# A two-block transformer kernel: the keys of differential attention projected 512 features at a time, and three smaller edits of pools and order

## The chip, the core and the metric

The kernel runs on one core of one Trainium2 chip. The metric is the device time of one execution in microseconds, as the median of several runs. TensorE (PE) multiplies, VectorE (DVE), ScalarE (ACT) and GpSimd (POOL) work element by element, and SyncE (SP) issues most of the transfers. Each engine runs its own list of instructions in order, and semaphores make one wait for another.

## The reference, cut to what matters

Two blocks follow each other on 512 tokens of 1024 features, all in fp32. The first is a DiT block: an RMS norm modulated by a condition, one input projection, a gated linear attention (GLA) and a differential attention side by side, an output projection, a second norm and a SwiGLU FFN. The second is a mixer block with a pooling and a "fox" attention branch, a cross attention to 256 memory tokens, and a FFN with a short convolution. The part that is projected differently here is `dk`, the keys of differential attention, for 256 context tokens and 512 tokens of x; the others keep their arithmetic.

```
def diff_qkv(parts, q_norm_g, k_norm_g):
    dq, dk, dv = parts[5:]
    ...
    k = rmsnorm(dk.reshape(b, n, DIFF_HEADS, 2, DIFF_DH).transpose(0, 2, 1, 3, 4), k_norm_g)
...
        x = x + gt1 * mix
        x = x + gt2 * swiglu(modulate(x, norm2_g[l], sh2, sc2), w_ffn_in[l], w_ffn_out[l])
```

## The kernel before, in words

Every large product is done as three matmuls on split operands (high by high, high by low, low by high). `wsplit` (L173) loads a chunk of 128x1024 weights into one of two `wf` buffers of a ring, casts its high part on ACT (L187) and subtracts the low part on DVE (L188); `whi` and `wlo` come from a small ring as well. A scheduler writes the order of each engine's list: by priorities, in the order in which the code issues work, with `tc.cur_priority` and `tc.issue_after` as corrections. Pools give memory, and a tile that takes the place of an older one waits for the older one's last reader.

The start is `normed_x` (L427): for four pairs of rows of x, ACT squares one into `t`, DVE squares the other into `u` and adds them (L433, L434), and PE sums over partitions (L313), with a few warming matmuls between. `t` has two buffers, `u` has one. Then come the modulation (L353), the spread of the norm factor (L332) and the first projections (L196 to L198).

The projections that have tokens as output rows are cut into tiles of 128 tokens by 256 features: `tm_job` (L674) loads the weights of half the features (two chunks) and runs 24 matmuls of 256 columns for each of six token tiles. For `dk` that is twelve tiles; after each, `qk_piece` (L648) squares and sums the heads and applies gains and rotation, and after the sixth tile of a half a factor `r_qk` is worked out and multiplied in (L692). All these tiles are entries of the list `fillers`. `mem_sq` (L725) lies between them: it loads a piece of the memory tokens into a buffer with the tag "t2", and squares into one with the tag "t1", which `qk_piece` uses too. The first entries are run ahead of the GLA stage, the last `PJ` = 20 between its steps. Where the stage opens, its constants `LT` and `Lr` are loaded through the two `wf` buffers and cast on DVE (L828, L831).

Norm 2 (L1323) runs behind the output projection for two halves of the tokens: it sums squares on PE, works out the factor and spreads it, in steps that lie between pieces of projection (`yield`). Behind the mixer's cross attention, `post` (L1434) adds its normed result, held in `KV` for the second half of the tokens, to `X` (L1453). The second FFN's pool `fp2` then takes the place of the pools `xp` and `xt`, of which `KV` is a tile. `Fhi` and `Flo` in `fp2` take split weights first (L187, L188), later split results.

Of the kernel before, what the change touches and what calls it, by code (L numbers as in the profile page):

```python
# [20 lines left out]
S = 512  # L21
# [7 lines left out]
RW = 1088  # L29
GH = 0  # L30
FA, FG, FC, A0, GR, MU = 3.4, 2.5, 5.6, 2, 2, 12
PJ, FP = 20, 8
NF = 2
NWF = 2
T0 = 1
# [11 lines left out]
QP = (0,)  # L47
Q3 = 0
MG = 1
WU, WX, WW = 15, 1, 5  # L50
MV, W0 = (0, 1), 1
XG = 9
ML = 0
W4, W5 = 1, 1
W1, W2 = 2, 2
X2 = (0, 2, 4)
XR, DR = (1, 3, 5, 7), (1, 3, 5, 7)
# [23 lines left out]
def kernel(ctx: ExitStack, tc: tile.TileContext, a: dict, out: bass.AP, stop=None):  # L81
# [307 lines left out]
    with tc.tile_pool(name="st", bufs=1) as st, tc.tile_pool(name="st2", bufs=2) as st2:  # L389
# [37 lines left out]
        def normed_x(x):  # L427

            pt = mis()
            for k in range(0, KT, 2):  # L430
                t, u = (st2.tile([128, S], F32, tag=f"sqt{j}", name="sqt", bufs=2 - j) for j in range(2))
                A.activation(t, x[:, k], AF.Square)
                V.tensor_tensor(u, x[:, k + 1], x[:, k + 1], ALU.mult)  # L433
                V.tensor_tensor(u, u, t, ALU.add)  # L434
                with tc.issue_after(warm(WU if k == 0 else WX)):
                    last_warm[0] = sum_sq(pt, u, k == 0, k == KT - 2)
            yield
            rb = st.tile([128, S], F32, tag="rbx", name="rbx")
# [206 lines left out]

    sums_of = {}

    def qk_piece(p, dst, gname, rope_t, key, i, n):  # L648


        if i == 0:
            sums_of[key] = mid2.tile([128, n, 4], F32, tag="qss", name="qss")
        sq = mid2.tile([128, 256], F32, tag="t1", name="qsq")
        A.activation(sq, p, AF.Square)  # L654
        V.tensor_reduce(sums_of[key][:, i], sq.rearrange("p (h e) -> p h e", h=4), AX, ALU.add)
        d4, p4 = dst.rearrange("p (h e) -> p h e", h=4), p.rearrange("p (h e) -> p h e", h=4)
        if rope_t is None:
            V.tensor_tensor(d4, p4, r_(gname).rearrange("p (o d) -> p o d", o=1).to_broadcast([128, 4, 64]), ALU.mult)
            return
        t2 = mid2.tile([128, 4, 2, 32], F32, tag="t2", name="t2")  # L660
        cs = cs64
        V.tensor_tensor(d4, p4, cs[:, 0, rope_t].rearrange("p (o d) -> p o d", o=1).to_broadcast([128, 4, 64]), ALU.mult)
        V.tensor_tensor(t2, p.rearrange("p (h y f) -> p h y f", h=4, y=2)[:, :, ::-1],
                        cs[:, 1, rope_t].rearrange("p (o y f) -> p o y f", o=1, y=2).to_broadcast([128, 4, 2, 32]), ALU.mult)
        V.tensor_tensor(d4, d4, t2.rearrange("p h y f -> p h (y f)"), ALU.add)

    def qk_rms(key, n):

        return rsqrt(mid2, sums_of[key].rearrange("p t h -> p (t h)"), 4 * n, 1.0 / 64, "qk")

    fillers = []
    got = {}
# [11 lines left out]
            take(hf, t, p[:, :256], slice(hf * 256, (hf + 1) * 256))  # L684
        return run

    def take_k(hf, t, p, cs):
        qk_piece(p, kn[:, t, cs], "k_g", None if t < 2 else t - 2, "k", t, 6)
        if t == 5:
            r = qk_rms("k", 6)  # L690
            k4 = kn[:, :, cs].rearrange("p t (h e) -> p t h e", h=4)
            V.tensor_tensor(k4, k4, r.rearrange("p (t h o) -> p t h o", t=6, o=1).to_broadcast([128, 6, 4, 64]), ALU.mult)  # L692

    late = {}

# [13 lines left out]
        if t == 5:  # L709
            V.tensor_scalar(rq[:, :, 4 * hf:4 * hf + 4], qk_rms("q", 4).rearrange("p (t h) -> p t h", t=4), 0.125, None, ALU.mult)  # L710

    jobs = [("w_dk", hf, range(6), take_k) for hf in range(2)]
    jobs += [("w_dv", hf, range(2), take_v) for hf in range(2)]
    jobs += [("w_dq", hf, range(2, 6), take_q) for hf in range(2)]
    jobs += [("w_dv", hf, range(2, 6), take_v) for hf in range(2)]
    for w, hf, ts_, take in jobs:
        if (w, hf) == ("w_dv", 0) and len(fillers) == 12:
            fillers.append((0.0, turn_q))
        for t in ts_:
            fillers.append((1.45, tm_job(w, hf, t, take, t == ts_[0])))  # L720
# [16 lines left out]
        V.tensor_copy(rm, r)  # L737
        bcast(rbm, r)
    for k in range(KT):
        fillers.insert(2 * k + 1, (0.0, lambda k=k: mem_sq(k)))  # L740
    fillers.insert(2 * KT + 2, (0.5, mem_stats))
    got_rs = []

    def silu_r(m, x, y, p):
# [71 lines left out]

    fill_to(len(fillers) - PJ)
    late_by[0] = HO
    gla_scope = ExitStack()
    gp = gla_scope.enter_context(tc.tile_pool(name="gp", bufs=1))  # L820
    gt = gla_scope.enter_context(tc.tile_pool(name="gt", bufs=2))
# [346 lines left out]
        mnl = mlo[:, 4:8].rearrange("p k (u t) -> p (k u) t", u=2)  # L1168

    gd = midp.tile([128, 1], F32, name="gd")  # L1170
    V.tensor_scalar(gd, col("diff_norm_g", 0), 0.8, None, ALU.mult)

    def mem_in(k):
        m = ap2.tile([128, MEM], F32, tag="mk", name="mk")
# [148 lines left out]
    def norm2(x, y):  # L1323
        for _ in range(W4 if x else W5):
            yield
        r = fm_stats(sp, sqs[:, x:y], "n2")
        for _ in range(3 if x else 1):
            yield
        bcast(rb[:, x:y], r)
        for k in range(KT):  # L1330
            if k % 2:
                yield
            t = sp.tile([128, S // 2], F32, tag="n2t", name="n2t")
            V.tensor_tensor(t, X[k][:, x:y], rb[:, x:y], ALU.mult)
# [99 lines left out]
    def post(Y, gname, nextg, g2, tails, spread):  # L1434


        def ev(m, x, y, p):
            V.tensor_scalar(Y(m // 2 * 2, x, y)[:, m % 2], p, col(gname, m), None, ALU.mult)
            add_sq(p, m, x, y)

        def after(x, y):
            rbp = sp.tile([128, S // 2], F32, tag="rbp", name="rbp")
            r = fm_stats(sp, sqs[:, x:y], "post")
            yield
            bcast(rbp, r)
            yield
            rb2 = rbp.rearrange("p (o t) -> p o t", o=1).to_broadcast([128, 2, S // 2])
            held = hq.tile([128, 2, S // 2], F32, tag="hld", name="hld")
            for k in range(0, KT + 2, 2):
                if k < KT:  # L1450
                    y2, x2 = Y(k, x, y), XT[k // 4][:, k % 4:k % 4 + 2, x:y]
                    V.tensor_tensor(y2, y2, rb2, ALU.mult)
                    V.tensor_tensor(x2, x2, y2, ALU.add)  # L1453
                    for j in (k, k + 1):
                        A.activation(g2[0][:, j, x:y], X[j][:, x:y], AF.Copy, scale=col(nextg, j))
                    t = held if k == 0 else sp.tile([128, 2, S // 2], F32, tag="sqx", name="sqx", bufs=1)
                    A.activation(t, x2, AF.Square)
                    yield
                if k > 0:
                    for j in (k - 2, k - 1):  # L1460
                        V.scalar_tensor_tensor(g2[1][:, j, x:y], X[j][:, x:y], col(nextg, j), f32(g2[0][:, j, x:y]),
                                               ALU.mult, ALU.subtract)
                    if k > 2:
                        V.tensor_tensor(held, held, last, ALU.add)
                    yield
                if k < KT:
                    last = t

            def tail():
# [213 lines left out]
    xa = ExitStack()  # L1683
    xp = xa.enter_context(tc.tile_pool(name="xp", bufs=1))
    xt = xa.enter_context(tc.tile_pool(name="xt", bufs=2))
    KV = xp.tile([128, 8, MEM], F32, name="KV")
    KVM, VM = KV[:, 0:4], KV[:, 4:8].rearrange("p (t u) n -> p t (u n)", t=2)
    g4 = new_q()
    Ym = xp.tile([128, KT, S], F32, name="Ym")
# [213 lines left out]
def _layout(i):  # L1903
# [68 lines left out]
```

## Time and profile before

| what | value |
|---|---|
| median of 3 runs | 1642.4 us (1641.32 to 1644.54) |
| the profiled execution: its time, its span | 1641.52 us, 1639.1 us |
| mean granted clock of PE over the span | 0.989 |
| DVE busy, ACT busy | 948.0 us (58%), 718.7 us (44%) |
| SP's queue of transfers | 158.15 MB |

The span is from the first to the last instruction; 2.4 us of the execution's time lie around it. Shares are of the span.

### The profile page before, as it was taken

How to read it: one execution, taken by the hardware profiler on the slowest of the kernel's cores; microseconds unless marked ns; L12 is line 12 of the kernel's file. 1: busy time of each engine (PE TensorE's matmuls, PEld its weight loads, DVE VectorE, ACT ScalarE, POOL GpSimd, SP SyncE). 2: the span in 40 equal slices, each digit the busy share in tenths (PEclk: the TensorE clock that was granted, in tenths of full speed). 3: DMA queues.
4: the chain of work that ended last, by engine and by line, in shares of the span. 5: the costliest groups of instructions: out<-in, count | busy, mean ns of one | idle time of the engine just before them, and what ended most of it. 6: DMA issues, size and time to landing. Idle time of an engine off the chain costs nothing.

```text
span 1639.1 us, 25459 instructions
## 1 busy us (share of the span) xinstructions
PE 1590.6 (97%) x10098; PEld 1355.6 (83%) x10098; DVE 948.0 (58%) x1791; ACT 718.7 (44%) x1353; POOL 214.1 (13%) x237
## 2 busy tenths in 40 slices
PE   7999999999999999999999999999998999999997
PEld 5798977778889888888889777888988988888887
DVE  5626898788765222223335676445788777776333
ACT  3424555677645323232223565224466544444221
POOL 0300000111022122210004000122000222221001
PEclk8999999999999999999999999999999999999999
DMA  8232245332322333333332212234211233323332
GB/s 350 82 89 78 66 158 180 124 100 78 128 88 78 103 94 99 91 99 94 93 114 72 77 39 65 91 103 148 84 52 34 83 93 100 103 90 97 97 93 74
DMA packets 49046, 163.23 MB, mean 100 GB/s; under 512 B 5664, under 2 KB 11296, under 8 KB 47392
## 3 DMA queue, kind: packets, MB, share of 16 engines
q1 hardware_dynamic: 45328, 158.15, 30.4%
q10 hardware_dynamic: 3312, 3.18, 0.6%
q8 instruction: 79, 1.29, 0.3%
q0 software_dynamic: 288, 0.28, 0.1%
q14 instruction: 39, 0.32, 0.1%
HBM read 158.72 MB, written 3.15 MB: 99 GB/s over the span
## 4 chain that ended last, share of the span: by engine, by line
PE 85%; DVE 5%; ACT 3%; DMA 1%; issue 1%; POOL 0%; ACTq 0%; DVEq 0%; POOLq 0%
PE acc L197 16%; PE acc L198 16%; PE acc L196 16%; PE s L198 5%; PE s L196 5%; PE s L197 5%; PE acc L286 3%; PE acc L285 3%; PE acc L287 3%; PE mis L1147 1%; PE mis L1632 1%; DVE wlo L188 1%; PE acc L775 1%; PE s L1118 1%; DMA mk<-in_memT 1%
## 5 line engine op out<-in xcount | busy, mean ns | idle before, releaser
L187 ACT CAST whi<-wf 128x1024 fp32r<-128x1024 f32 (+4 forms) x221 | 228.6, 1034 | 422.6 <-PE acc L197 277.7
L188 DVE TENSOR_TENSOR wlo<-wf,whi 128x1024 fp32r<-128x1024 f32 (+2 forms) x183 | 222.0, 1213 | 176.2 <-ACT whi L187 172.3
L196 PE MATMUL acc<-qhi,whi 128*128 128x512 f32 (+1 forms) x640 | 239.4, 374 | 0.0
L197 PE MATMUL acc<-qlo,whi 128*128 128x512 f32 (+1 forms) x640 | 239.3, 374 | 0.0
L198 PE MATMUL acc<-qhi,wlo 128*128 128x512 f32 (+1 forms) x640 | 239.3, 374 | 0.0
L196 PEld LDWEIGHTS acc<-qhi,whi 128*128 128x128 f32 x640 | 120.8, 189 | 19.6
L197 PEld LDWEIGHTS acc<-qlo,whi 128*128 128x128 f32 x640 | 120.7, 189 | 19.7 <-issue 0.2
L198 PEld LDWEIGHTS acc<-qhi,wlo 128*128 128x128 f32 x640 | 120.7, 189 | 19.3
L196 PE MATMUL s<-qhi,whi 128*128 128x512 f32 (+1 forms) x336 | 128.3, 382 | 0.0
L198 PE MATMUL s<-qhi,wlo 128*128 128x512 f32 (+1 forms) x336 | 128.3, 382 | 0.0
L197 PE MATMUL s<-qlo,whi 128*128 128x512 f32 (+1 forms) x336 | 128.2, 382 | 0.0
L188 POOL TENSOR_TENSOR wlo<-wf,whi 128x1024 fp32r<-128x1024 f32 x38 | 91.0, 2396 | 214.3 <-ACT whi L187 214.3
L1417 DVE TENSOR_TENSOR e<-e,s 128x512 f32<-128x512 f32 (+1 forms) x22 | 14.3, 651 | 154.2 <-PE s L198 154.1
L197 PE MATMUL acc<-glo,whi 128*128 128x512 f32 (+1 forms) x208 | 74.4, 358 | 0.1
L196 PE MATMUL acc<-ghi,whi 128*128 128x512 f32 (+1 forms) x208 | 74.4, 358 | 0.0
L198 PE MATMUL acc<-ghi,wlo 128*128 128x512 f32 (+1 forms) x208 | 74.2, 357 | 0.0
L196 PEld LDWEIGHTS s<-qhi,whi 128*128 128x128 f32 x336 | 64.0, 190 | 11.9
L197 PEld LDWEIGHTS s<-qlo,whi 128*128 128x128 f32 x336 | 64.0, 190 | 11.8
L198 PEld LDWEIGHTS s<-qhi,wlo 128*128 128x128 f32 x336 | 63.9, 190 | 11.8
L197 PE MATMUL acc<-Flo,whi 128*128 128x512 f32 (+1 forms) x187 | 71.6, 383 | 0.0
L285 PE MATMUL acc<-whi,hhi 128*128 128x256 f32 (+1 forms) x224 | 67.1, 299 | 3.4 <-ACT qsq L654 2.5
L286 PE MATMUL acc<-wlo,hhi 128*128 128x256 f32 (+1 forms) x224 | 65.6, 293 | 3.3 <-DVE wlo L188 3.3
(648 smaller groups left out, 3833.4 us busy)
## 6 DMA issues: line engine op xcount, KB each, us to landing
wf<-in_w_ffn_in SPq DMA_DIRECT2D x44, 512.0 KB, 3.6
wf<-in_w_up SPq DMA_DIRECT2D x44, 512.0 KB, 3.5
wm<-in_w_mod SPq DMA_DIRECT2D x32, 512.0 KB, 3.6
wm<-in_w_mod SPq DMA_DIRECT2D x8, 1024.0 KB, 11.7
wf<-in_w_ffn_out SPq DMA_DIRECT2D x16, 512.0 KB, 3.5
wf<-in_w_g SPq DMA_DIRECT2D x16, 512.0 KB, 3.5
wf<-in_w_down SPq DMA_DIRECT2D x16, 512.0 KB, 3.5
wf<-in_w_dv SPq DMA_DIRECT2D x8, 512.0 KB, 3.7
```

What stands on the lines that cost most here:

```text
L187: A.copy(hi[:, :n], wf[:, :n])
L188: (lo_eng or V).tensor_tensor(lo[:, :n], wf[:, :n], f32(hi[:, :n]), ALU.subtract)
L196: T.matmul(o, lhi, rhi, start=start, stop=False)
L197: T.matmul(o, lhi, rlo, start=False, stop=False)
L198: ins = T.matmul(o, llo, rhi, start=False, stop=stop).ins
L285: T.matmul(o, bhi(k), whi, start=k == 0, stop=False)
L286: T.matmul(o, bhi(k), wlo, start=False, stop=False)
L287: T.matmul(o, blo(k), whi, start=False, stop=k == KT - 1)
L775: T.matmul(p[32 * j:32 * j + 32, :256], silc[:, 4 * kc + j], wf[:, j * 256:(j + 1) * 256], start=kc == 0, stop=kc == 1, skip_group_check=T ...
L1118: T.matmul(s_[:, n0:n1], QF[:, c, ts], KA[:, c, n0:n1], start=True, stop=False)
L1147: T.matmul(p[:, :128], aT[:, kt * 128:(kt + 1) * 128], v, start=kt == 0, stop=kt == NKT - 1)
L1632: T.matmul(pO[:, ts], vz[:, kt, hp_, 64 * e:64 * e + 128], pT[:, kt * 128:(kt + 1) * 128], start=kt + e == 0, stop=kt - t + e == 1, skip_g ...
```

## The change

The keys' weights are loaded as four chunks of two contraction steps by all 512 features, split, and kept in a pool of their own (`wd`) for all six token tiles; each tile is 24 matmuls of 512 columns, and `qk_piece` works on 512 features with buffers of its own. The factor is worked out once at the end, and multiplied in with two instructions. The pools `wd` and `wd2` close where the GLA stage opens. `PJ` and the places of `mem_sq` follow the new list. In `normed_x`, `u` has two buffers, there are two warming matmuls fewer, and `gd` is issued after the first projections have started. Norm 2's second half takes its sums one step later and spreads one step earlier, and the additions to `X` ahead of it get a higher priority. `KV` moves to the pool `hq`, which stays; `rbp` shares the tag "n2t".

```diff
-PJ, FP = 20, 8
+PJ, FP = 15, 8
...
-WU, WX, WW = 15, 1, 5
+WU, WX, WW = 13, 1, 5
...
-W4, W5 = 1, 1
+W4, W5 = 2, 1
...
-                t, u = (st2.tile([128, S], F32, tag=f"sqt{j}", name="sqt", bufs=2 - j) for j in range(2))
+                t, u = (st2.tile([128, S], F32, tag=f"sqt{j}", name="sqt", bufs=2) for j in range(2))
...
-    def qk_piece(p, dst, gname, rope_t, key, i, n):
+    def qk_piece(p, dst, gname, rope_t, key, i, n, pool=None):
+        ng = p.shape[-1] // 64
+        pool = pool or mid2
...
-        sq = mid2.tile([128, 256], F32, tag="t1", name="qsq")
+        sq = pool.tile([128, 64 * ng], F32, tag="t1", name="qsq")
...
+    wide_scope = ExitStack()
+    wd = wide_scope.enter_context(tc.tile_pool(name="wd", bufs=1))
+    wd2 = wide_scope.enter_context(tc.tile_pool(name="wd2", bufs=2))
+    wide = []
+
+    def wide_load(j):
+        hi, lo = (wd.tile([128, 1024], F32R, name=f"wide{j}{i}") for i in range(2))
+        wide.append(wsplit(a["w_dk"][j].rearrange("p k n -> p (k n)"), 1024, dst=(hi, lo, None)))
+
+    def k_job(t):
+        def run():
+            p = acc()
+            x, i = ((chi, clo), t) if t < 2 else ((hx, hxl), t - 2)
+            for k in range(KT):
+                if len(wide) == k // 2:
+                    wide_load(k // 2)
+                hi, lo = wide[k // 2]
+                sl = slice(k % 2 * 512, k % 2 * 512 + 512)
+                xh_, xl_ = tok(x[0], i)(k), tok(x[1], i)(k)
+                T.matmul(p, xh_, hi[:, sl], start=k == 0, stop=False)
+                T.matmul(p, xh_, lo[:, sl], start=False, stop=False)
+                T.matmul(p, xl_, hi[:, sl], start=False, stop=k == KT - 1)
+                if k % 2 and k < KT - 1:
+                    yield
+            qk_piece(p, kn[:, t], "k_g", None if t < 2 else t - 2, "k", t, 6, wd2)
+            if t == 5:
+                r = qk_rms("k", 6, wd2)
+                r6 = r.rearrange("p (t h o) -> p t h o", t=6, o=1)
+                for t0 in (0, 3):
+                    k4 = kn[:, t0:t0 + 3].rearrange("p t (h e) -> p t h e", h=8)
+                    V.tensor_tensor(k4, k4, r6[:, t0:t0 + 3].to_broadcast([128, 3, 8, 64]), ALU.mult)
+        return run
...
-    jobs = [("w_dk", hf, range(6), take_k) for hf in range(2)]
-    jobs += [("w_dv", hf, range(2), take_v) for hf in range(2)]
+    for t in range(6):
+        fillers.append((1.36, k_job(t)))
+    jobs = [("w_dv", hf, range(2), take_v) for hf in range(2)]
...
-        fillers.insert(2 * k + 1, (0.0, lambda k=k: mem_sq(k)))
-    fillers.insert(2 * KT + 2, (0.5, mem_stats))
+        fillers.insert(k + k // 2 + 1, (0.0, lambda k=k: mem_sq(k)))
+    fillers.insert(KT + 6, (0.5, mem_stats))
...
     fill_to(len(fillers) - PJ)
     late_by[0] = HO
+    wide_scope.close()
...
-    V.tensor_scalar(gd, col("diff_norm_g", 0), 0.8, None, ALU.mult)
+    with tc.issue_after(hid):
+        V.tensor_scalar(gd, col("diff_norm_g", 0), 0.8, None, ALU.mult)
...
-        for _ in range(3 if x else 1):
+        for _ in range(2 if x else 1):
...
         for m, (p, _, _) in enumerate(parts):
+            tc.cur_priority -= 2 * WO
             V.scalar_tensor_tensor(X[m], p, mods[:, 16 + m, 0:1], X[m], ALU.mult, ALU.add)
+            tc.cur_priority += 2 * WO
...
-    KV = xp.tile([128, 8, MEM], F32, name="KV")
+    KV = hq.tile([128, 8, MEM], F32, name="KV")
```

Three places in the engines' lists show what moves. The first is DVE's list in the first norm, from the first square on; `sqt` is the square, L1171 is `gd`. Before:

```order
L433 TENSOR_TENSOR sqt<-X_97 128x512
L411 TENSOR_TENSOR silc<-cT,silc 128x256
L434 TENSOR_TENSOR sqt<-sqt 128x512
L125 CAST identr<-ident 128x128
L1171 TENSOR_SCALAR gd<-cols 128x1
L433 TENSOR_TENSOR sqt<-X_97 128x512
L434 TENSOR_TENSOR sqt<-sqt 128x512
L433 TENSOR_TENSOR sqt<-X_97 128x512
L434 TENSOR_TENSOR sqt<-sqt 128x512
L433 TENSOR_TENSOR sqt<-X_97 128x512
L434 TENSOR_TENSOR sqt<-sqt 128x512
```

And in the changed kernel, where `gd` is L1203:

```order
L433 TENSOR_TENSOR sqt<-X_97 128x512
L411 TENSOR_TENSOR silc<-cT,silc 128x256
L434 TENSOR_TENSOR sqt<-sqt 128x512
L433 TENSOR_TENSOR sqt<-X_97 128x512
L434 TENSOR_TENSOR sqt<-sqt 128x512
L125 CAST identr<-ident 128x128
L433 TENSOR_TENSOR sqt<-X_97 128x512 x2
L434 TENSOR_TENSOR sqt<-sqt 128x512 x2
```

`gd`, which needs `cols`, no longer stands ahead of the second square, and the last two squares stand side by side.

The second is DVE's list where keys end. Before, this is the end of the first of the two halves: `qss` are the sums of a tile, L166 to L170 work out `r_qk`, L692 multiplies by it, and `wlo` belongs to the next chunks of weights:

```order
L188 TENSOR_TENSOR wlo<-wf,whi 128x1024
L733 TENSOR_TENSOR rows<-rows,mks 128x256
L655 TENSOR_REDUCE qss<-qsq 128x4
L662 TENSOR_TENSOR kdv<-acc,cs_99 128x256
L663 TENSOR_TENSOR t_1266<-acc,cs_99 128x256
L166 TENSOR_SCALAR v_qk<-qss 128x24
L665 TENSOR_TENSOR kdv<-kdv,t_1266 128x256
L168 SCALAR_TENSOR_TENSOR t_qk<-v_qk,y_qk 128x24
L169 TENSOR_TENSOR t_qk<-t_qk,y_qk 128x24
L170 SCALAR_TENSOR_TENSOR r_qk<-t_qk,y_qk 128x24
L692 TENSOR_TENSOR kdv<-kdv,r_qk 128x6x256
L733 TENSOR_TENSOR rows<-rows,mks 128x256
```

In the changed kernel it is the end of all keys; L720 is the multiply, `r_m` is the factor of the memory tokens that PE spreads next, and `wlo` belongs to the first chunks of `dv`:

```order
L166 TENSOR_SCALAR v_qk<-qss 128x48
L166 TENSOR_SCALAR v_m<-mis 128x2
L666 TENSOR_TENSOR kdv<-kdv,t_1297 128x512
L168 SCALAR_TENSOR_TENSOR t_qk<-v_qk,y_qk 128x48
L168 SCALAR_TENSOR_TENSOR t_m<-v_m,y_m 128x2
L169 TENSOR_TENSOR t_qk<-t_qk,y_qk 128x48
L169 TENSOR_TENSOR t_m<-t_m,y_m 128x2
L170 SCALAR_TENSOR_TENSOR r_qk<-t_qk,y_qk 128x48
L170 SCALAR_TENSOR_TENSOR r_m<-t_m,y_m 128x2
L720 TENSOR_TENSOR kdv<-kdv,r_qk 128x1536 x2
L767 COPY rm<-r_m 128x2
L188 TENSOR_TENSOR wlo<-wf,whi 128x1024 x2
```

The next weights' `wlo` stood ahead of the half's last tile, and now stands behind the two multiplies.

The third is ACT's list at the entry of the second FFN. Before, from the second half's `qhi` on (L1455), with `Fhi` behind them:

```order
L1455 ACTIVATE qhi<-X_5341,cols 128x256 x2
L1457 ACTIVATE hld<-X_5341 128x512
L1455 ACTIVATE qhi<-X_5341,cols 128x256 x2
L1457 ACTIVATE sqx<-X_5341 128x512
L333 COPY rb<-mis 128x256
L1455 ACTIVATE qhi<-X_5343,cols 128x256 x2
L1457 ACTIVATE sqx<-X_5343 128x512
L187 CAST Fhi<-wf 128x1024
L1794 ACTIVATE early<-z,cols 128x256 x2
L187 CAST Fhi<-wf 128x1024
L1455 ACTIVATE qhi<-X_5343,cols 128x256 x2
L1800 ACT_TABLE_LOAD
```

In the changed kernel, from the squares of the last cross attention tile on (L1340, L1343):

```order
L1340 ACTIVATE sqs<-acc 128x256
L1343 ACTIVATE sqt<-acc 128x256 x6
L187 CAST Fhi<-wf 128x1024
L1343 ACTIVATE sqt<-acc 128x256
L187 CAST Fhi<-wf 128x1024
L165 ACTIVATE y_post<-mis,epsc 128x2
L167 ACTIVATE y_post<-y_post 128x2
L165 ACTIVATE y_pre<-sums,epsc 128x2
L167 ACTIVATE y_pre<-y_pre 128x2
L333 COPY rbp<-mis 128x256
L333 COPY rb<-mis 128x256
L187 CAST Fhi<-wf 128x1024
```

The first `Fhi` casts now stand ahead of the factor `y_post` and of all `qhi`, which are L1489 here and stand behind these rows.

## Rows read from the trace of the kernel before

**Rows 1.** Page, part 1: busy time, share of the span, instructions.

```profile
PE 1590.6 (97%) x10098; PEld 1355.6 (83%) x10098; DVE 948.0 (58%) x1791; ACT 718.7 (44%) x1353; POOL 214.1 (13%) x237
```

**Rows 2.** Waits of PE over the whole span: total us, times, longest us.

```profile
PE s L196 <- ACT Fhi L187: 4.5, 1, 4.5
PE acc L286 <- DVE wlo L188: 3.3, 2, 2.9
PE acc L285 <- ACT qsq L654: 2.5, 1, 2.5
PE mis L313 <- DVE sqs L1312: 2.2, 1, 2.2
...
PE acc L196 <- DVE X L1343: 1.9, 1, 1.9
...
PE acc L285 <- DVE v_qk L166: 1.0, 1, 1.0
```

**Rows 3.** Windows: busy us (instructions) by engine, then PEclk, the granted clock.

```profile
12.60:22.80 10.20, 8.10 (x43) 6.47 (x44) 3.16 (x9) 0.84 (x3) 0.00 (x0) 0.50 1.02 413
70.60:74.00 3.40, 3.40 (x17) 3.40 (x17) 2.53 (x6) 2.10 (x5) 0.00 (x0) 0.50 0.51 164
138.90:142.30 3.40, 3.40 (x18) 3.40 (x17) 0.43 (x1) 0.42 (x1) 0.00 (x0) 0.50 0.03 5
490.50:493.90 3.40, 3.40 (x18) 3.40 (x17) 1.70 (x4) 2.57 (x5) 0.00 (x0) 0.50 0.46 133
1265.30:1272.10 6.80, 4.80 (x20) 4.51 (x21) 6.75 (x14) 6.33 (x10) 2.35 (x7) 0.50 0.32 84
```

**Rows 4.** Timeline of the start, DVE: start us, us, instruction, [idle before <-releaser].

```profile
9.40 0.15 DVE L1171 TENSOR_SCALAR gd<-cols 128x1 f32<-128x1 f32 x1 [2.52 <-DMA cols<-in_cols]
...
12.16 0.69 DVE L433 TENSOR_TENSOR sqt<-X 128x512 f32<-128x512 f32 x1 [1.17 <-PE mis L313]
...
16.46 0.69 DVE L434 TENSOR_TENSOR sqt<-sqt 128x512 f32<-128x512 f32 x1
```

**Rows 5.** Timeline of the start, PE.

```profile
17.20 1.92 PE L313 MATMUL mis<-ones,sqt 128*128 128x32 f32 x8 [1.00 <-DVE sqt L434]
...
26.60 0.51 PE L196 MATMUL s<-hhi,whi 128*128 128x512 f32 x1 [0.86 <-ACT hhi L381]
```

**Rows 6.** Timeline, DVE, ahead of the second gv weight chunk.

```profile
63.49 0.75 DVE L383 TENSOR_TENSOR hc<-mc,hc 128x256 fp32r<-128x256 f32 x2
...
69.04 1.28 DVE L188 TENSOR_TENSOR wlo<-wf,whi 128x1088 fp32r<-128x1088 f32 x1
```

**Rows 7.** Timeline, PE: neighbours of 512 columns, then of 256.

```profile
38.23 0.39 PE L196 MATMUL s<-hhi,whi 128*128 128x512 f32 x1
38.46 0.39 PE L197 MATMUL s<-hlo,whi 128*128 128x512 f32 x1
...
156.23 0.28 PE L287 MATMUL acc<-whi,hc 128*128 128x256 f32 x1
156.35 0.28 PE L285 MATMUL acc<-whi,hc 128*128 128x256 f32 x1
```

**Rows 8.** Timeline, DVE, in the k stage.

```profile
116.94 0.63 DVE L828 CAST LT<-lt 128x896 fp32r<-128x896 f32 x1 [1.68 <-DMA lt<-in_LT]
...
131.07 0.41 DVE L655 TENSOR_REDUCE qss<-qsq 128x4 f32<-128x256 f32 x1
...
133.18 1.76 DVE L692 TENSOR_TENSOR kdv<-kdv,r_qk 128x1536 f32<-128x1536 f32 x1
```

**Rows 9.** Page, part 6, DMA issues: xcount, KB each, median us to landing.

```profile
wf<-in_w_dv SPq DMA_DIRECT2D x8, 512.0 KB, 3.7
```

**Rows 10.** Timeline, DVE, norm 2's second half.

```profile
488.71 0.42 DVE L1312 TENSOR_TENSOR sqs<-sqs,sqt 128x256 f32<-128x256 f32 x1
```

**Rows 11.** Timeline, ACT, entry of the second FFN.

```profile
1265.74 1.04 ACT L187 CAST Fhi<-wf 128x1024 fp32r<-128x1024 f32 x1 [0.97 <-DVE X L1453]
...
1269.54 1.28 ACT L1800 ACT_TABLE_LOAD   x1
```

More of the change, by code (lines that the diff above doesn't have):

```diff
@@ L646 @@
     sums_of = {}
-    def qk_piece(p, dst, gname, rope_t, key, i, n):
+    def qk_piece(p, dst, gname, rope_t, key, i, n, pool=None):
+        ng = p.shape[-1] // 64
+        pool = pool or mid2
         if i == 0:
-            sums_of[key] = mid2.tile([128, n, 4], F32, tag="qss", name="qss")
-        sq = mid2.tile([128, 256], F32, tag="t1", name="qsq")
+            sums_of[key] = pool.tile([128, n, ng], F32, tag="qss", name="qss")
+        sq = pool.tile([128, 64 * ng], F32, tag="t1", name="qsq")
@@ L654, in qk_piece @@
         A.activation(sq, p, AF.Square)
-        V.tensor_reduce(sums_of[key][:, i], sq.rearrange("p (h e) -> p h e", h=4), AX, ALU.add)
-        d4, p4 = dst.rearrange("p (h e) -> p h e", h=4), p.rearrange("p (h e) -> p h e", h=4)
+        V.tensor_reduce(sums_of[key][:, i], sq.rearrange("p (h e) -> p h e", h=ng), AX, ALU.add)
+        d4, p4 = dst.rearrange("p (h e) -> p h e", h=ng), p.rearrange("p (h e) -> p h e", h=ng)
         if rope_t is None:
-            V.tensor_tensor(d4, p4, r_(gname).rearrange("p (o d) -> p o d", o=1).to_broadcast([128, 4, 64]), ALU.mult)
+            V.tensor_tensor(d4, p4, r_(gname).rearrange("p (o d) -> p o d", o=1).to_broadcast([128, ng, 64]), ALU.mult)
@@ L659, in qk_piece @@
             return
[L660 to L664, printed above, removed]
+        t2 = pool.tile([128, ng, 2, 32], F32, tag="t2", name="t2")
@@ L665, in qk_piece, with qk_rms @@
+        V.tensor_tensor(d4, p4, cs64[:, 0, rope_t].rearrange("p (o d) -> p o d", o=1).to_broadcast([128, ng, 64]), ALU.mult)
+        V.tensor_tensor(t2, p.rearrange("p (h y f) -> p h y f", h=ng, y=2)[:, :, ::-1],
+                        cs64[:, 1, rope_t].rearrange("p (o y f) -> p o y f", o=1, y=2).to_broadcast([128, ng, 2, 32]), ALU.mult)
         V.tensor_tensor(d4, d4, t2.rearrange("p h y f -> p h (y f)"), ALU.add)
-    def qk_rms(key, n):
-        return rsqrt(mid2, sums_of[key].rearrange("p t h -> p (t h)"), 4 * n, 1.0 / 64, "qk")
+    def qk_rms(key, n, pool=None):
+        v = sums_of[key].rearrange("p t h -> p (t h)")
+        return rsqrt(pool or mid2, v, v.shape[-1], 1.0 / 64, "qk")
@@ L685, in tm_job @@
         return run
[L687 to L692, printed above, removed]
+    wide_scope = ExitStack()
[28 more added lines that the diff above has]
+        return run
     late = {}
@@ L716 @@
     for w, hf, ts_, take in jobs:
-        if (w, hf) == ("w_dv", 0) and len(fillers) == 12:
+        if (w, hf) == ("w_dv", 0) and len(fillers) == 6:
             fillers.append((0.0, turn_q))
@@ L1441, in after @@
         def after(x, y):
-            rbp = sp.tile([128, S // 2], F32, tag="rbp", name="rbp")
+            rbp = sp.tile([128, S // 2], F32, tag="n2t", name="rbp")
             r = fm_stats(sp, sqs[:, x:y], "post")
@@ L1932, in _layout @@
     o["w_dq"], o["w_dk"], o["w_dv"] = (_tmw(w[:, 1568 + 512 * j + f]) for j, f in enumerate((halves, halves, np.arange(512))))
+    o["w_dk"] = w[:, 2080 + halves].reshape(4, 2, 128, 512).transpose(0, 2, 1, 3)
     gu = np.zeros((128, 4, 2, 64), np.float32)
```

## The prediction

> **What bounds the kernel now.** The page's first part comes first: PE is busy 97% of the span [rows 1], and no other engine is near that. So time can go only where PE waits, or where it runs slower than it could. The second view is the list of PE's waits by what ended them [rows 2]: the largest one that ends on a single instruction is 4.5 us for the cast `Fhi` at the second FFN, then 2.9 for a `wlo` and 2.5 for a `qsq` in the projections, 2.2 for norm 2's sums, 1.9 for an addition to `X`, 1.0 for `v_qk`. The third is the granted clock. Over the span it is 0.989, but five stretches at the places of this change have 0.50, the lower of PE's two levels (1.2 against 2.4 GHz) [rows 3]. Four of them lie where a wait of rows 2 has just ended (2.9, 2.5, 2.2 and 4.5 us), the first lies in the stop-and-go of the first norm. PE that is busy in such a stretch loses half of its length: 1.7 us for 3.40 us, 3.4 us for 6.80. So each of these waits has cost its length and then some. Every edit of this change touches one of these places, and I price them in order of time, against the profiled execution of 1641.5 us.
>
> **First norm.** `gd` stands ahead of the second square on DVE and held it 2.52 us, until 9.40, for `cols` [rows 4]; then `u`, with one buffer, made each square wait for PE's sum of the pair before (1.17 us before 12.16) [rows 4]. The last add began at 16.46 and the last sum at 17.20 [rows 4, 5]. Without both, DVE can go on at 9.40-2.52 = 6.88. X is issued ahead of `cols` on the same queue, so I take it that all of X is there by 9.40. If it is there when wanted, six operations of 0.69 end at 11.0; if the last two pairs come only at 9.40, four more operations end at 12.2. Before it was 16.46+0.69 = 17.15. That is 5.0 to 6.1 us; I take 5.5. The first projection matmul at 26.60 [rows 5] hangs on the last sum through the norm factor and `hhi`, so it moves along. It could gain more, up to 7, if the last sum runs at full clock (its 1.92 us lie in a stretch at 0.50 [rows 3, 5]). It gains less if weights bind: the transfers are saturated there (DMA share 1.02 [rows 3]), and their landings don't move with the norm. As the upper end I take the wait at `gd` alone, 2.5. Term: **-5.5** (-7 to -2.5). The two warming matmuls fewer lie in PE's wait for the first sum and cost nothing; if they didn't, they would be worth 0.2 us.
>
> **gv's second weight chunk.** Its `wlo` at 69.04 stood on DVE behind eight `hc` subtractions that began at 63.49 [rows 6], and PE waited 2.9 us. In the changed lists it stands ahead of them: -2.9 and -1.7 for the stretch at 70.6. But ACT's list now has the cast of the first wide chunk ahead of the cast of gv's last one. That one may come late by a `wlo` (1.28 [rows 6]), a transfer (3.7 [rows 9]) and a cast (1.04 [rows 11]), together 6.0, or by nothing if PE has enough tiles to do. I take the nearest wait for such an operand, 2.9 [rows 2]. Term: **-1.7** (-4.6 to +1.4).
>
> **The keys.** Columns: two neighbours of 512 stand 0.23 us apart, two of 256 stand 0.12 apart [rows 7]. 288 matmuls at 0.12 are 34.6 us, 144 at 0.23 are 33.1: -1.4. The trace decides against a rule of the Trainium skill here, which speaks against the change: "TensorE: Matmul & The Clock Gate", section "Back-to-back issue gap", gives a spacing of columns / 2.4 + 2.5 ns for a single stream; that would be an estimate of 109 and 216 ns, 31.4 against 31.1 us, and a gain of 0.3 instead of 1.4.
>
> The waits for `qsq` and `v_qk` inside the stage go: -2.5 and -1.0 [rows 2], and -1.7 for the stretch at 138.9 [rows 3]. `qsq` was held by ACT behind the memory squares, whose buffers the tiles shared; now they have their own.
>
> What comes is at the end. `LT` takes the memory of the wide tiles, so its cast waits for PE's last k matmul, at a time T. Behind it on DVE are the last tile's work, the two factors, and then the two multiplies, all ahead of the `wlo` that the first `dv` tile needs. Before, sums to multiply took 133.18-131.07 = 2.1 us for 256 columns [rows 8]; four long operations of double width add some 4x0.33 and four short ones for `r_m` 4x0.2, so 4.2. With the casts of `LT` (0.63 [rows 8]) and `Lr` (some 0.4) ahead, PE gets `r_m` at T+5.2, and the `wlo` ends two multiplies of 1.76 [rows 8] and 1.28 later, at T+10.0. PE's own work in between (sums, spread, two gate products) is about ten times 0.23, so the hole is at most 7.7; successive operations of DVE overlap a little, so I take 6.5, and a stretch at half clock behind it, +1.7. `LT` and `Lr` also hold both `wf` buffers until T, so the first `dv` chunk lands at T+0.6+3.7 and is cast at T+5.4: earlier than its `wlo` can start, hence hidden by the multiplies. Sum: -1.4-2.5-1.0-1.7+6.5+1.7 = **+1.6** (-2.6 with a hole of 4 and no stretch, +5.8 with 9 and twice the stretch).
>
> **GLA and attention.** The list has 15 entries left instead of 20 when GLA begins, so PE may run out of fill in one of its steps. The sum of PE's work is unchanged. I take +0.5, between nothing and one wait like that at `X`, 1.9 [rows 2]. Term: **+0.5** (0 to +1.9).
>
> **Norm 2.** The last addition to the sums began at 488.71 [rows 10], and PE waited 2.2 us for it [rows 2] with the stretch at 490.5 behind. One step later means one more piece of projection ahead of the sums, 24 matmuls of 256 columns or 24x0.12 = 2.9 us: it covers the wait. -2.2-1.7 = **-3.9** (-3.9 to 0; without that cover the 2.2 stays, and the factor would come late as well). The priority of the additions to `X` moves the second one past a subtraction, but the third, which ended the wait of 1.9, still stands behind the same `wlo` in the changed list: 0 (-1.2 to 0).
>
> **The second FFN.** ACT's `Fhi` at 1265.74 waited for `X` at L1453 [rows 11], the last reader of `KV`, whose place `Fhi` takes. With `KV` elsewhere the cast stands ahead of the whole factor and `qhi` work, and its weights are long there. -4.5, and -3.4 for the stretch at 1265.3. The changed list has one ACT table load more in this stage, 1.28 us [rows 11], between factor and gelu, and I charge it in full: PE works on early tiles there whose results come back through ACT. Term: **-6.6** (-7.9 if the load is hidden, -3.2 if the clock falls here anyway).
>
> **Sum.** -5.5-1.7+1.6+0.5-3.9-6.6 = -15.6, so 1625.9 against the profiled 1641.5. The median shown is 0.9 above that execution: **1626.8 us**. From the terms' bounds, the likely case runs from 1621 to 1632.
>
> **The rivals.**
> - The clock doesn't come back. Three stretches that I count as gone (gv, norm 2, FFN: 1.7+1.7+3.4 = 6.8) stay, because shorter waits are left at the same places. For it: the stretch at 138.9 follows a wait of 2.5 us like those that I leave in. Against: no stretch follows the wait of 1.9 at `X` [rows 2, 3]. 1626.8+6.8 = 1633.6.
> - The page's spacing holds in the new shape. The wide tiles then gain 0.3 instead of 1.4: 1627.9. The rows show 0.23 and 0.12 in this kernel's own streams, so little speaks for it.
> - The stalls only move. The waits removed are 4.5+2.9+2.5+2.2+1.0 = 13.1 us; PE runs in order, so the next late operand (`dv`'s `wlo`, `qhi` of the FFN's second half) may take most of them. With the start's 5.5 given back to the saturated transfers too, some 2 us are left: 1640.
> - The hole at the keys' end turns into a slow stage: slower. PE stops and goes from T through GLA's opening, where every gate product waits for DVE, and the clock stays at 0.50. Without the keys the terms are -17.2, so it decides when hole and clock together cost 17.2+3.3+6.6 = 27.1 instead of 8.2: the hole of 7.7 and some 39 us at half clock. For it: the stop-and-go of the start stayed at 0.50 for 10.20 us [rows 3]. Against: no stretch in the trace is longer. With 45 us it gives about 1650.
>
> **How the numbers follow.** 0.2%, 3.3 us, is about what a measurement of this kernel can tell from no change. Chances: the forecast 0.60, the clock 0.20, the page's spacing 0.05, moved stalls 0.09, the slow stage 0.06. The first three are faster, 0.85; the fourth is the same, 0.09; the last slower, 0.06. The range holds the likely case and the clock's: 1618 to 1637.
>
> **What would show it.** In the changed trace: the last sum of the first norm at about 11.5, the first projection near 21; no wait of PE for `wlo` near 65 to 70, but one for `whi` or `wlo` of gv's last chunk; 512-column k matmuls at 0.23; a wait of PE for `r_m` and then for `wlo`, 6 to 7 us in sum, behind the last of them; no wait for `sqs` at norm 2 and none for `Fhi` at the FFN, and no 0.50 at these two. The prediction is wrong if the first projection stays later than 23, if the hole is over 10 us, or if PE waits at the FFN for something else as long as it did for `Fhi`.

## The result and the profile after

| | median | range | runs |
|---|---|---|---|
| before | 1643.72 us | 1641.32 to 1644.54 | 5 |
| changed | 1634.22 us | 1631.75 to 1637.36 | 5 |

The ratio is 0.9948, 95% interval 0.9930 to 0.9965: 9.5 us faster, where 15.6 were forecast. The execution profiled took 1636.76 us (span 1635.0, granted clock 0.989), 4.8 less than the one profiled before, so its trace shows half of the gain. The five executions differ in the clock: 0.988 and 0.989 in the two longest, 0.992 in the two shortest, and 0.003 of 1635 is 4.9 us.

PE's waits in the changed kernel, as in [rows 2]; lines have moved by some 30:

```profile
PE mis L332 <- DVE r_m L170: 4.0, 1, 4.0
PE acc L285 <- ACT whi L187: 3.0, 2, 2.0
PE acc L197 <- DVE mlo L1209: 2.8, 3, 1.5
PE acc L805 <- DMA wm<-in_w_mod: 2.8, 5, 0.8
...
PE acc L196 <- issue: 1.8, 1, 1.8
PE mis L911 <- DVE ktc L904: 1.8, 1, 1.8
...
PE acc L196 <- DVE z L1824: 1.4, 1, 1.4
PE mis L313 <- DVE sqt L434: 1.4, 2, 1.1
...
PE acc L286 <- DVE wlo L188: 0.8, 1, 0.8
...
PE mis L313 <- DVE sqs L1344: 0.3, 1, 0.3
```

Of the six rows of [rows 2], `Fhi`, `qsq`, `v_qk`, the `wlo` of 2.9 and the 2.2 for `sqs` are gone (0.3 is left of the last), and the 1.9 at `X` is still there: it is the row of 1.8 that the trace puts down to "issue". New are the waits for `r_m`, for a `whi`, for `ktc`, for `mlo` in attention, for modulation weights, and the 1.4 for `z` at the second FFN.

The second view answers to [rows 3]: stretches, with PE's busy time first and the granted clock after POOL's.

```profile
87.50:90.90 3.40, 3.40 (x17) 3.40 (x16) 0.17 (x1) 1.03 (x2) 0.00 (x0) 0.51 0.72 271
142.30:149.10 6.80, 5.29 (x13) 3.16 (x14) 6.80 (x14) 4.26 (x7) 1.94 (x2) 0.52 0.66 200
159.30:162.70 3.40, 3.40 (x19) 3.40 (x19) 0.82 (x2) 0.46 (x2) 0.00 (x0) 0.53 0.35 135
336.70:343.50 6.80, 5.30 (x19) 4.31 (x19) 5.37 (x12) 5.14 (x11) 0.00 (x0) 0.51 0.24 78
460.10:463.50 3.40, 3.40 (x21) 3.40 (x20) 2.14 (x4) 1.40 (x2) 0.00 (x0) 0.59 0.66 220
488.00:500.00 12.00, 11.71 (x97) 11.43 (x97) 9.30 (x21) 7.00 (x15) 2.98 (x3) 1.00 0.55 176
1255.00:1290.00 35.00, 34.59 (x285) 33.89 (x283) 28.27 (x64) 25.04 (x45) 6.72 (x15) 1.00 0.21 61
```

At norm 2 (488 to 500) and at the second FFN (1255 to 1290) the clock is 1.00, as forecast. The five stretches at some 0.5 above these two rows are at places that were clean before. They cost 1.7, 3.4, 1.7, 3.4 and 1.7 us, some 12, more than the four that went (138.9, 70.6, 490.5 and 1265.3 in [rows 3], 8.5). The start lost less, in the first 26 us and in the 34 behind them; the kernel before comes first, the changed one second:

```profile
0.00:26.00 26.00, 18.98 (x122) 16.08 (x122) 11.01 (x25) 7.24 (x13) 1.29 (x10) 0.80 0.93 371
26.00:60.00 34.00, 30.87 (x199) 20.02 (x200) 22.41 (x53) 15.18 (x30) 9.41 (x9) 0.95 0.59 212
```

```profile
0.00:26.00 26.00, 20.28 (x126) 16.16 (x127) 15.14 (x30) 9.42 (x15) 1.29 (x10) 0.87 0.93 368
26.00:60.00 34.00, 32.56 (x220) 22.32 (x219) 22.60 (x57) 17.11 (x34) 10.37 (x11) 1.00 0.63 229
```

That is 0.07 of 26 us and 0.05 of 34 us, some 3.5 us more. So the two profiled executions lose about as much by the clock, some 12 against 12, and both have 0.989 over the span.

Three marks on PE show where the profiled pair gains and loses. At the first projection the changed kernel is 4.5 us ahead; at the first gate product of x in GLA it is 1.0 behind (165.15 against 164.19); at the out projection's kept weights `kh`, ahead of norm 2, it is 4.4 behind (458.57 against 454.16). What it gains over the whole span it gains at norm 2 and at the second FFN. The third mark, before and then changed:

```profile
454.16 0.36 PE L196 MATMUL acc<-mhi,kh 128*128 128x256 f32 x1 [1.88 <-DVE X L1343]
```

```profile
458.57 0.36 PE L196 MATMUL acc<-mhi,kh 128*128 128x256 f32 x1 [1.84 <-issue]
```

The first norm, on DVE and then on PE, against [rows 4, 5]:

```profile
7.01 0.69 DVE L433 TENSOR_TENSOR sqt<-X 128x512 f32<-128x512 f32 x1 [0.18 <-DMA X<-in_xT]
...
9.67 0.69 DVE L433 TENSOR_TENSOR sqt<-X 128x512 f32<-128x512 f32 x1 [0.43 <-PE mis L313]
10.28 1.29 DVE L434 TENSOR_TENSOR sqt<-sqt 128x512 f32<-128x512 f32 x2
```

```profile
12.23 1.69 PE L313 MATMUL mis<-ones,sqt 128*128 128x32 f32 x8
...
22.07 0.50 PE L196 MATMUL s<-hhi,whi 128*128 128x512 f32 x1 [0.86 <-ACT hhi L381]
```

The square that stood behind `gd` now starts at 7.01, the last sum at 12.23 instead of 17.20, the first projection at 22.07 instead of 26.60.

gv's last chunk, on ACT and on PE, against [rows 6]:

```profile
83.59 1.04 ACT L187 CAST wide<-wf 128x1024 fp32r<-128x1024 f32 x1 [3.98 <-DMA wf<-in_w_dk]
84.54 1.09 ACT L187 CAST whi<-wf 128x1088 fp32r<-128x1088 f32 x1
```

```profile
85.69 0.39 PE L285 MATMUL acc<-whi,hc 128*128 128x272 f32 x1 [1.95 <-ACT whi L187]
```

ACT's cast of the first wide chunk stood 3.98 us for its transfer, and gv's `whi`, which needs no transfer any more, behind it. PE waited 1.95 us for that `whi`, and 0.8 for its `wlo`.

The end of the keys, on DVE, ACT and PE, against [rows 7, 8]; the last k matmul started at 139.04:

```profile
139.48 0.63 DVE L859 CAST LT<-lt 128x896 fp32r<-128x896 f32 x1 [2.37 <-PE acc L711]
...
143.51 0.15 DVE L170 SCALAR_TENSOR_TENSOR r_m<-t_m,y_m 128x2 f32<-128x2 f32 x1
143.63 3.43 DVE L720 TENSOR_TENSOR kdv<-kdv,r_qk 128x1536 f32<-128x1536 f32 x2
...
147.04 2.88 DVE L188 TENSOR_TENSOR wlo<-wf,whi 128x1024 fp32r<-128x1024 f32 x2
```

```profile
143.83 1.05 ACT L187 CAST whi<-wf 128x1024 fp32r<-128x1024 f32 x1 [2.15 <-DMA wf<-in_w_dv]
```

```profile
133.21 0.39 PE L710 MATMUL acc<-wide,hhi 128*128 128x512 f32 x1
133.44 0.39 PE L711 MATMUL acc<-wide,hlo 128*128 128x512 f32 x1
...
139.04 0.40 PE L711 MATMUL acc<-wide,hlo 128*128 128x512 f32 x1
...
143.81 1.20 PE L332 MATMUL mis<-ident,r_m 128*128 128x128 f32 x4 [4.00 <-DVE r_m L170]
144.80 3.62 PE L885 MATMUL mis<-gu,cg__600 128*128 128x512 f32 x4
```

The columns are as forecast: 0.23 us from one wide matmul to the next. `LT`'s cast began the moment that PE was through with the wide tiles, `r_m` came 4.2 us later, the multiplies took 3.43, and `wlo` followed at 147.04. PE waited 4.00 us, and then ran the four gate products at half speed, 3.62 us: the clock was 0.52 until 149.1. So there was no further wait for that `wlo`; the half clock had used it up.

The FFN's first `Fhi` cast, against [rows 11]:

```profile
1255.95 1.05 ACT L187 CAST Fhi<-wf 128x1024 fp32r<-128x1024 f32 x1 [0.47 <-PE acc L198]
```

What ended ACT's idle time ahead of it is a matmul of PE, nothing of `X`, and it starts 9.8 us earlier.

### The profile page after: what moved, and what is told of

Same layout as the page of the kernel before. It is cut to its first block, busy times and chain, and to the rows that moved or that the text cites. A ratio compares the mean times of both kernels' runs of the same rounds, so it can differ in the third digit from the quotient of the medians.

```text
span 1635.0 us, 25114 instructions
## 1 busy us (share of the span) xinstructions
PE 1590.7 (97%) x9950; PEld 1347.4 (82%) x9950; DVE 943.5 (58%) x1767; ACT 716.3 (44%) x1346; POOL 213.6 (13%) x237
## 4 chain that ended last, share of the span: by engine, by line
PE 84%; DVE 4%; DMA 3%; ACT 3%; issue 2%; POOL 1%; ACTq 0%; DVEq 0%; POOLq 0%; SPq 0%
PE acc L197 16%; PE acc L196 16%; PE acc L198 16%; PE s L198 5%; PE s L196 5%; PE s L197 5%; PE acc L286 2%; PE acc L285 2%; PE acc L287 2%; PE mis L1178 1%; PE mis L1666 1%; PE acc L805 1%; DMA wm<-in_w_mod 1%; PE s L1149 1%; PE mis L1170 1%
## 5 line engine op out<-in xcount | busy, mean ns | idle before, releaser
L187 ACT CAST whi<-wf 128x1024 fp32r<-128x1024 f32 (+4 forms) x217 | 224.2, 1033 | 425.2 <-PE acc L197 286.3
L188 DVE TENSOR_TENSOR wlo<-wf,whi 128x1024 fp32r<-128x1024 f32 (+3 forms) x179 | 218.9, 1223 | 173.7 <-ACT whi L187 169.8
L1829 DVE SCALAR_TENSOR_TENSOR zc<-z,cols,zc 128x512 f32<-128x512 f32 (+1 forms) x44 | 50.1, 1139 | 19.8 <-ACT zc L1828 19.4
L285 PE MATMUL acc<-whi,hhi 128*128 128x256 f32 (+1 forms) x160 | 47.2, 295 | 1.1 <-ACT whi L187 1.1
```

The costliest lines, as they stand in the source:

```text
L187: A.copy(hi[:, :n], wf[:, :n])
L188: (lo_eng or V).tensor_tensor(lo[:, :n], wf[:, :n], f32(hi[:, :n]), ALU.subtract)
L285: T.matmul(o, bhi(k), whi, start=k == 0, stop=False)
L1829: V.scalar_tensor_tensor(t, z[:, 1 + x:1 + y], col("conv_w1", j), t, ALU.mult, ALU.add)
```

## The experiments

Two theories to begin with. K: the small edits hold, and the keys' edit itself costs what is missing. M: waits and half-clock stretches move on, whatever the keys do. All runs below were timed in turn with the kernel before; ratios, with 95% intervals in brackets, are to it.

**The three small edits without the keys', and the keys' alone.** `e1` is the kernel before with the lines of the diff on `WU`, `u`, `gd`, `W4`, the yields, the priority, `rbp` and `KV`; `e2` has all the others.

> The kernel before with the first norm's, norm 2's and the FFN pool's edits, and the keys as before in twelve tiles of 256. Theory K (the keys' edit itself costs some 6 us, by the hole at its end and by what it leaves to GLA and attention): the three small edits keep -5.8, -3.2 and -6.4 of the profiled pair, so 15 us below before, about 1628, and faster than the full change. Theory M (the small gains are taken back by waits and half-clock stretches that move into attention whatever the keys do): about 1634, as the full change.

> The kernel before with the keys' edit alone (wide tiles, PJ, places of mem_sq, wide pool closed ahead of GLA). Theory K: slower than before by 4 to 7 us, about 1648, with the wait for r_m of some 4 us and half clock behind the last k tile, and 2 to 5 us more lost in attention. Theory M: within 3 us of before, 1641 to 1645.

Measured: `e1` 1627.17 us, 0.9899 (0.9878 to 0.9920), faster than the full change; `e2` 1648.80, 1.0033 (1.0021 to 1.0044), 5 us slower than before. That speaks for K, except for the losses in attention that it names: from the first gate product of x to `kh`, `e2` takes 290.1 us where before it was 290.0. In `e2` both the hole and the old wait for gv's `wlo` stand in PE's waits from 60 to 172 us:

```profile
PE mis L332 <- DVE r_m L170: 4.0, 1, 4.0
PE acc L286 <- DVE wlo L188: 3.4, 2, 2.9
```

`e1` shows what M has right: it has no half clock at norm 2 or the FFN, but a new stretch in GLA (first row), which costs (1-0.66)*5 = 1.7 us, and another from 911 to 916 us, also at 0.66.

```profile
225.00:230.00 5.00, 4.04 (x26) 2.69 (x26) 4.61 (x10) 0.58 (x2) 0.00 (x0) 0.66 0.47 168
488.00:500.00 12.00, 12.00 (x102) 12.00 (x102) 9.77 (x22) 8.51 (x19) 7.10 (x8) 1.00 0.39 121
1255.00:1290.00 35.00, 33.58 (x260) 32.42 (x260) 29.78 (x66) 24.98 (x43) 7.52 (x17) 1.00 0.19 62
```

**Each small edit alone.**

```diff
-    KV = xp.tile([128, 8, MEM], F32, name="KV")
+    KV = hq.tile([128, 8, MEM], F32, name="KV")
```

> The kernel before with KV in the pool hq and rbp under the other tag, nothing else. Both theories: no wait of PE for Fhi and no half clock at 1265, -6.4 us, about 1636.5. If the wait only moves to another operand of the second FFN: 1640 or more.

`e3` measured 1637.77 us, 0.9966 (0.9954 to 0.9978): 5.6 us faster by the ratio, 5.9 by the medians. The wait for `Fhi` is gone, and one of 1.4 for `z` has come.

```diff
-... name="sqt", bufs=2 - j) for j in range(2))
+... name="sqt", bufs=2) for j in range(2))
...
+    with tc.issue_after(hid):
```

> The kernel before with the second buffer for u, gd issued later and 13 warming matmuls. Theory K: the first projection 5 to 6 us earlier, and all of it kept to the end: about 1637. Theory M: 3 us or more are given back by the end of attention, 1640 or more.

`e4` measured 1635.42 us, 0.9955 (0.9942 to 0.9967): 7.4 to 8.2 us, more than the norm itself. Its trace says why: gv's `wlo` is no longer behind the `hc` subtractions, though the keys are as before.

```profile
57.51 1.29 DVE L188 TENSOR_TENSOR wlo<-wf,whi 128x1088 fp32r<-128x1088 f32 x1 [0.70 <-ACT whi L187]
...
61.81 0.75 DVE L383 TENSOR_TENSOR hc<-mc,hc 128x256 fp32r<-128x256 f32 x2
```

So the wait of 2.9 at gv [rows 2] goes by the first norm's edit, not by the new list; in `e2`, without that edit, it stayed.

```diff
-W4, W5 = 1, 1
+W4, W5 = 2, 1
...
-        for _ in range(3 if x else 1):
+        for _ in range(2 if x else 1):
```

> The kernel before with norm 2's edits alone (sums one step later, spread one step earlier, priority of the additions to X). By the profiled pair -3.2 us, about 1640.5; no wait of PE for sqs at 489 and no half clock behind it, the wait of 1.9 at X unchanged. If the sums only fall into the next late operand: 1643 or more.

`e5` measured 1641.03 us, 0.9986 (0.9973 to 0.9999): 2.3 us by the ratio, 3.5 by the medians, and the interval barely leaves out no change. In its trace the wait for `sqs` at 489 is gone and the one at `X` is still 1.8.

**What in the keys' edit costs.** Theory H: the hole at the keys' end. Theory L: a list with less left for GLA and attention.

```diff
-PJ, FP = 15, 8
+PJ, FP = 20, 8
```

> The changed kernel with 20 entries of the list left for GLA instead of 15. Theory L (GLA and attention cost 7 us more because the list has less to fill their steps with): 3 to 6 us faster than the changed kernel, 1628 to 1631, with fewer waits in attention. Theory H (the hole at the keys' end is the cost, and the rest follows from it): same as the changed kernel, 1632 to 1636.

`e6` measured 1637.82 us, 0.9964 (0.9950 to 0.9978): if anything slower than the changed kernel. L as stated falls; its trace has waits in attention that the changed kernel hasn't:

```profile
PE mis L1109 <- issue: 5.4, 1, 5.4
PE mis L1051 <- ACT AT L1043: 2.1, 1, 2.1
```

It is no support for H either. PE has other tiles to run at the keys' end, doesn't wait for `r_m`, and waits 1.4 us from 110 to 172 where the changed kernel waits 5.8; yet the time is no shorter, because from 318 to 460 the waits rise from 7.4 to 14.0 us and the clock is 0.93 instead of 0.97.

```diff
-    fillers.insert(KT + 6, (0.5, mem_stats))
+    fillers.insert(KT + 5, (0.5, mem_stats))
```

> The changed kernel with the memory tokens' factor worked out ahead of the last k tile instead of behind it. Theory H: the wait for r_m of 4.0 us behind the last k matmul goes, PE runs the gate products in that time and then waits for dv's wlo at T+8.8, so 1 to 3 us faster, 1631 to 1633. If the wait for the wlo takes all of it: no change, 1634.

`e7` measured 1633.31 us, 0.9936 (0.9917 to 0.9956), not told apart from the changed kernel. The wait for `r_m` is gone, but from 110 to 172 us PE waits for `dv`'s weights instead, first the cast, then the `wlo`:

```profile
PE acc L285 <- ACT whi L187: 4.1, 1, 4.1
PE acc L286 <- DVE wlo L188: 2.2, 1, 2.2
```

```diff
+                tc.cur_priority += 300
                 for t0 in (0, 3):
...
+                tc.cur_priority -= 300
```

> As the run before, and one of the two multiplies by r_qk stands behind dv's first wlo on DVE. Theory H: the wlo is 1.7 us earlier too, the hole falls from 4.0 us and 6.8 us of half clock to 2 us or less: 4 to 7 us faster than the changed kernel, 1627 to 1630. Theory L: 2 us at most.

`e8` measured 1632.70 us, 0.9936 (0.9915 to 0.9957). The wait for `wlo` falls to 0.5 us, the 4.1 for the cast stays, and nothing is gained that the interval can tell. H as I had put it, a matter of DVE's list, was too narrow. The cast waits for a transfer, which waits for a `wf` buffer, and both buffers are held by `LT` and `Lr`, whose casts wait for the wide tiles' memory. In the changed kernel's trace SP stands 40.9 us for the cast of `Lr`, and only then issues `dv`'s first transfers:

```profile
140.13 0.81 SPq L178 DMA_DIRECT2D wf<-in_w_dv  x2
```

So the next experiment takes away what they wait for, memory, and another the wait at gv:

```diff
+    ltp = lt_scope.enter_context(tc.tile_pool(name="ltp", bufs=1))
+    LT = ltp.tile([128, NLEV * 128], F32R, name="LT")
+    Lr = ltp.tile([128, 4, 128], F32R, name="Lr")
     wide_scope = ExitStack()
...
-    LT = gp.tile([128, NLEV * 128], F32R, name="LT")
-    Lr = gp.tile([128, 4, 128], F32R, name="Lr")
```

> The changed kernel, with LT and Lr in a small pool of their own below the wide tiles (and one t2 buffer less to make room), so that their casts and the release of both wf buffers don't wait for PE's last k matmul. Theory H2 (the hole has three layers, r_m, dv's transfer and dv's wlo, and all three hang on those two buffers and on DVE's list behind the casts): the hole of 4.0 + 1.8 us of waits and some 5 us of clock goes for the most part, 4 to 8 us faster than the changed kernel, 1626 to 1630. Rival (another operand takes the place, as in the two runs with the factor moved): 1632 or more.

`e10` measured 1628.98 us, 0.9909 (0.9893 to 0.9926). `LT` is cast at 99.7 there, and SP begins to issue `dv`'s transfers at 100.35. PE's busy time, other engines and clock from 110 to 172 us, the changed kernel first and this one second:

```profile
110.00:172.00 62.00, 56.22 (x296) 47.16 (x295) 35.48 (x60) 21.98 (x41) 4.71 (x4) 0.92 0.24 70
```

```profile
110.00:172.00 62.00, 61.84 (x372) 53.96 (x371) 38.26 (x67) 22.55 (x45) 3.86 (x4) 1.00 0.22 60
```

From 56.22 us busy at a clock of 0.92 to 61.84 at 1.00; one wait of 0.2 us is left there:

```profile
PE acc L285 <- ACT kdv L736: 0.2, 1, 0.2
```

For gv, the first wide chunk's cast is issued after gv's last one:

```diff
+            with tc.issue_after(src_at.pop()):
+                A.copy(hi[:, :n], wf[:, :n])
```

> The changed kernel, with ACT's cast of gv's last chunk ahead of the cast of the first wide chunk (order of two instructions on ACT and on DVE). Theory Q (of the keys' cost, some 4.5 us are this cast behind a transfer that it doesn't need: waits of 2.0 and 0.8 and a stretch at half clock): 3 to 5 us faster than the changed kernel, 1629 to 1631. Rival (the first k tile then waits as long for its first wide chunk): no change, 1633 or more.

`e9` measured 1630.79 us, 0.9923 (0.9908 to 0.9938): 3.4 us faster than the changed kernel by the medians, though the two intervals overlap. Both waits at gv's last chunk are gone and the first wide tile waits for nothing.

> Both edits of the two runs before. If both theories hold: 1622 to 1626, as fast as or faster than the small edits without the keys' edit (1627). If the keys' cost lies in GLA and attention: 1630 or more.

`e11` measured 1623.15 us, 0.9876 (0.9861 to 0.9891), the fastest of all and below `e9` and `e10`, whose intervals lie above its own. PE from 60 to 172 us is busy 110.88 of 112, at full clock:

```profile
60.00:172.00 112.00, 110.88 (x753) 101.88 (x752) 66.31 (x123) 48.75 (x95) 8.13 (x12) 1.00 0.29 87
```

> The run before, with the memory tokens' factor ahead of the last k tile and one multiply by r_qk behind dv's wlo as well. If something of the hole is left at the keys' end: 1 to 3 us faster than 1623. If LT's place was all of it: the same, 1622 to 1625.

`e12` measured 1625.30 us, 0.9885 (0.9866 to 0.9905), range 1621.18 to 1628.56: not told apart from the run before. What was to be had at the keys' end was `LT`'s place.

## Why the prediction was right, and where its sum was too good

The time lies in the range and the direction was right; the gain was 0.6 of the one forecast. By its own steps:

**First norm.** Right: 5.0 us at the last sum, 4.5 at the first projection, for -5.5. The sums ran at half clock again (12.23 to some 14, in a stretch that lasts until 19.2), so the further gain that I named as a bound did not come. That the first projection lies ahead of 23, my own sign of being right, is not firm: in `e1`, with the same first norm, it starts at 23.86.

**gv.** The old wait went, though by the first norm's edit and not by the changed lists, as `e4` and `e2` show. The new one was named and sized well: 2.0+0.8, for 2.9. But I did not give it the half-clock stretch that I gave to the others; it had one, 1.7 us at 87.5. The term was nothing, not -1.7. `e9` takes the new waits away, and `e11` shows the gain clear of the intervals: 5.8 us below `e10`.

**The keys.** The columns came as forecast, 0.23 us apart, so the wide tiles gain what the rows of before had. The rule of the Trainium skill ("TensorE: Matmul & The Clock Gate", section "Back-to-back issue gap") that I had put against it gives 0.216 and 0.109 as an estimate. The trace shows 0.23 and 0.12. I took the rule for one on streams, but the section gives it for an isolated matmul; for a stream of weight loads and matmuls it gives some 0.131 us at 512 columns, and no stream here comes near that.

The hole was there, but in part another one. The wait for `r_m` came, 4.0 us. The wait for `dv`'s `wlo` that I had behind it did not; instead PE waited 1.8 for `ktc` until 158.70, which stood on DVE behind the `wlo` of `dv`'s next transfers, issued at 148.29. In sum 5.8 for 6.5. The term that was mis-sized is the clock behind it, which I put at 1.7: two stretches, 6.8 us and 3.4 us, cost 5.1. That `dv`'s first transfer is "hidden by the multiplies" held in this kernel: it was cast by 144.88, ahead of its `wlo` at 147.04. But being hidden is not being free. It was late on its own account, by two `wf` buffers held until T, and showed itself as soon as `r_m` was moved (`e7`, `e8`). With that and the wait at gv out of the way, in `e11`, the wide keys are worth some 4 us (1623.15 against the 1627.17 of `e1`, with intervals that overlap a little), where the gains of my working came to 6.6.

**GLA and attention.** I put 0.5, at most 1.9; the profiled execution lost 3.4, 293.4 us against 290.0 from the first gate product of x to `kh`. The list's length is not shown to be the cause: theory L's experiment failed, and over the same way the kernels with the keys as before take 290.0 to 294.9 (293.1 in `e1`), those with wide keys 290.1 to 295.0 (290.6 in `e11`). Two things come with the wide keys all the same, and no run here says why. PE waits 2.0 to 2.9 us in all for `mlo` in attention in each of the nine profiles with wide keys, and at most 0.2 in the five others. And from 320 to 350 us the clock is 0.67 to 0.94 in the eight profiles that have the small edits too, among them that of `e11`, and 1.00 in the other six.

**Norm 2 and FFN.** Right in mechanism, both waits and both stretches gone. Norm 2's spread stays at its step; the sums alone move, one step nearer to it. Sizes: 2.3 to 3.5 for 3.9, 5.6 to 5.9 for 6.6. I named no wait that would take the place of `Fhi`; there was one, 1.4 for `z`.

**The sum.** The small edits were put at 5.5+4.6+3.9+6.6 = 20.6 with gv's old wait; `e1` measured 16.5. The keys with gv's new wait and GLA were put at 1.6+2.9+0.5 = 5.0; the changed kernel is 7.0 slower than `e1`. So 4.1 of the 6.1 us that are missing lie in the small edits: alone they gave 7.4 to 8.2 for 10.1 (first norm with gv's old wait), and norm 2 and the FFN what stands above. The other 2.0 lie in the keys, gv's new wait and GLA. The profiled execution shows more there than 2.0: 3.4 more of half clock at the keys' end, 1.7 more at gv and 2.9 more in GLA and attention, against 0.7 less of waits. But it is 2.5 us longer than the median, and the other executions have no trace, so how the 2.0 divide is not shown.

The rival on the clock gave 1633.6, near the 1634.2 measured, but not by its mechanism: the stretches that it kept at norm 2 and the FFN went. Others came, behind the new waits or with a cause that isn't known, and in the profiled pair the clock as a whole did not come back, 0.989 in both. That the number fits is in part luck. What I should have counted is every wait that the change leaves or makes, with its stretch, not only those that it removes.

## What to carry to other kernels

A pool opened in the place of one that PE is still reading ties its first tiles to PE's last read, and with them everything that those tiles hold: here two staging buffers of the weights' ring, so a transfer of another stage. 5.5 kilobytes per partition moved aside (and one buffer of `t2` given up for them) were worth 5 us (1634.2 to 1629.0); reordering DVE's list ahead of the late transfer was worth nothing that could be told. And when a wait is priced, price the clock behind it too, on the side of the losses as on that of the gains.

## What the hardware showed unasked

Of one program, five executions spread over 5.6 us with the granted clock between 0.988 and 0.992. The kernel before does the same when it is run more often: its 27 executions beside `e1` to `e4` lie between 1640.13 and 1649.32 us, with the clock between 0.985 and 0.991. Where the clock falls is not decided by a wait's length alone: the wait at `X` has a stretch at half clock behind it in the changed kernel's profiled execution (1.8 us, then 460.1), and had none in the one profiled before (1.9 us [rows 2]). It is no whim of one execution, either: of the fourteen profiles five have a stretch there, the changed kernel, `e2`, `e7`, `e8` and `e9`, which are all those with wide keys, a late `LT` and 15 entries left. `e10` to `e12`, with `LT` early, wait 2.0 to 2.2 us at that place and have none. Why stays open.
